# Scaling tokens by expert weights: one VectorE instruction per four tokens, named buffers, a fixed DMA order, and a first load split over two queues

## The chip, the cores and the metric

The kernel runs on one core of a Trainium2 chip. The metric is device time in microseconds (us) of one execution, as the median of several runs. The core's engines that matter here are VectorE (DVE in the profile), ScalarE (ACT) and SyncE (SP). ScalarE and SyncE also issue DMA transfers, each into a queue of its own; the transfers of both queues run on the core's 16 DMA engines.

## The reference, cut to what matters

```python
batch, seq, hidden, k = 16, 1024, 512, 2
# x: (16, 1024, 512) f32, expert_weights: (16, 1024, 2) f32; expert_indices is not used
x_expanded = x[:, :, np.newaxis, :].repeat(k, axis=2)
return (x_expanded * expert_weights[..., np.newaxis]).astype(np.float32)
```

There are 16,384 tokens of 512 numbers. Each token is written out twice, once times its first weight and once times its second. So 33.6 MB of x and 0.13 MB of weights are read, and 67.1 MB are written, with one multiplication for each number written.

## The kernel before, in words

**Tiling.** The 16,384 tokens are 128 per partition. They are taken in five groups of 24 tokens per partition and one of 8. Each group of 24 is cut into two tiles of 12 tokens, so there are eleven tiles, numbered 0 to 10 here: ten of 12 tokens per partition (3072 KB of x, 6144 KB of output) and a last one of 8 (2048 KB and 4096 KB). Inside a group a partition holds consecutive tokens, so that a tile's piece of x is 24,576 contiguous bytes per partition (16,384 in tile 10) and its output 49,152 (32,768 in tile 10).

**Buffers.** x has four buffers (`XB = 4`, line 31 and the pool in line 41), the output two (line 42). All weights lie in one tile, `w_tile`.

**Loads.** `load(i)` (lines 79 to 95) issues the load of tile i from ScalarE's queue. Tile 0 is cut into three pieces of four tokens (line 85), the others are one DMA each. After the first piece of tile 0 the weights of the first group are loaded (`first_weights`, line 56), and after its last piece all others (`other_weights`, lines 59 and 63). Lines 97 and 98 issue the loads of tiles 0 to 3 ahead. The load of tile i+4 stands in line 128, behind the work on tile i whose buffer it takes.

**Work.** For each token and each of its two weights there is one multiplication of 128x512 numbers by a scalar per partition: every third one goes to ScalarE (`nc.scalar.mul`, line 109), the other two to VectorE (`tensor_scalar`, line 115). That makes 85 on ScalarE and 171 on VectorE, 8 and 16 in a tile of 12 tokens.

**Stores.** When a tile is done, SyncE issues one store for it (line 124), eleven in all. An output buffer can be written again when the store before the last has landed.

**What sets the order.** The kernel is written with a layer that places each engine's instructions in an order of its own and adds the waits. Each engine and each queue then runs its instructions in that order: loads and ScalarE's multiplications share ScalarE's order, stores have SyncE's to themselves, and the order is not written by hand.

Of the kernel before, what the change touches and what calls it, by code (L numbers as in the profile page):

```python
# [1 line left out]

# [4 lines left out]


@with_exitstack
def kernel(  # L10
    ctx: ExitStack,
    tc: tile.TileContext,
    x: bass.AP,
    expert_indices: bass.AP,
    expert_weights: bass.AP,
    out: bass.AP,
):
    nc = tc.nc

    batch, seq, hidden = x.shape  # L20
    k = expert_weights.shape[-1]
    P = nc.NUM_PARTITIONS
    ntok = batch * seq
    assert ntok % P == 0
    A_TOTAL = ntok // P

    f32 = mybir.dt.float32
    row = k * hidden
    TX = 12
    TO = 12  # L30
    XB = 4

    groups = [[12, 12]] * 5 + [[8]]
    assert sum(sum(g) for g in groups) == A_TOTAL

    xf = x.rearrange("b s h -> (b s) h")
    of = out.rearrange("b s k h -> (b s) (k h)")
    wf = expert_weights.rearrange("b s k -> (b s) k")

    w_pool = ctx.enter_context(tc.tile_pool(name="w_pool", bufs=1))  # L40
    x_pool = ctx.enter_context(tc.tile_pool(name="x_pool", bufs=XB))
    o_pool = ctx.enter_context(tc.tile_pool(name="o_pool", bufs=2))

    w_tile = w_pool.tile([P, A_TOTAL * k], f32)

    def rows(of_all, done, T):
        return of_all[done * P : (done + T) * P, :].rearrange(
            "(p a) n -> p (a n)", a=T
        )

    T0 = sum(groups[0])
    G = len([g for g in groups[1:] if sum(g) == T0])
    head = (1 + G) * T0

    def first_weights():
        nc.scalar.dma_start(out=w_tile[:, : T0 * k], in_=rows(wf, 0, T0))  # L56

    def other_weights():
        nc.scalar.dma_start(  # L59
            out=w_tile[:, T0 * k : head * k].rearrange("p (g n) -> p g n", g=G),  # L60
            in_=wf[T0 * P : head * P, :].rearrange("(g p a) n -> p g (a n)", g=G, p=P),
        )
        nc.scalar.dma_start(  # L63
            out=w_tile[:, head * k :], in_=rows(wf, head, A_TOTAL - head)
        )

    tiles = []
    done = 0
    for group in groups:
        T = sum(group)  # L70
        a0 = 0
        for n in group:
            tiles.append((done, T, a0, n))
            a0 += n
        done += T

    loaded = []

    def load(i):
        if i >= len(tiles):  # L80
            return
        done, T, a0, n = tiles[i]
        x_tile = x_pool.tile([P, TX * hidden], f32)
        src = rows(xf, done, T)
        step = TX // 3 if i == 0 else n
        for at in range(0, n, step):
            nc.scalar.dma_start(  # L87
                out=x_tile[:, at * hidden : (at + step) * hidden],
                in_=src[:, (a0 + at) * hidden : (a0 + at + step) * hidden],
            )  # L90
            if i == 0 and at == 0:
                first_weights()
        if i == 0:
            other_weights()
        loaded.append(x_tile)

    for i in range(XB):
        load(i)
    for i, (done, T, a0, n) in enumerate(tiles):
        x_tile = loaded[i]  # L100
        outr = rows(of, done, T)
        for t in range(n):
            if t % TO == 0:
                o_tile = o_pool.tile([P, TO * row], f32)
            for kk in range(k):
                c = (done + a0 + t) * k + kk
                o = t % TO * row + kk * hidden
                if c % 3 == 2:
                    nc.scalar.mul(  # L109
                        out=o_tile[:, o : o + hidden],  # L110
                        in_=x_tile[:, t * hidden : (t + 1) * hidden],
                        mul=w_tile[:, c : c + 1],
                    )
                    continue
                nc.vector.tensor_scalar(  # L115
                    out=o_tile[:, o : o + hidden],
                    in0=x_tile[:, t * hidden : (t + 1) * hidden],
                    scalar1=w_tile[:, c : c + 1],
                    scalar2=None,
                    op0=mybir.AluOpType.mult,  # L120
                )
            if (t + 1) % TO == 0 or t + 1 == n:
                at = t // TO * TO
                nc.sync.dma_start(  # L124
                    out=outr[:, (a0 + at) * row : (a0 + t + 1) * row],
                    in_=o_tile[:, : (t + 1 - at) * row],
                )
        load(i + XB)

# [1 line left out]
_INS = ['x', 'expert_indices', 'expert_weights']  # L131
_OUTS = [((16, 1024, 2, 512), 'float32')]


# [23 lines left out]
```

## Time and profile before

| what | value |
|---|---|
| time, median of 3 runs | 240.93 us (240.92 to 242.47) |
| time of the profiled execution | 241.01 us |
| its span in the profile | 239.2 us (1.8 us lie around it) |
| VectorE busy | 68.8 us, 171 instructions |
| ScalarE busy | 54.7 us, 86 instructions (85 multiplications and a table load) |
| bytes moved by DMA | 100.82 MB, 421 GB/s over the span |
| loads of 3072 KB, issue to landing | 80.3 us (median of 9) |
| stores of 6144 KB, issue to landing | 31.4 us (median of 10) |

Times inside the profile are counted from the start of the span. The page gives busy times by engine, then the span in 40 slices with the mean busy share of the 16 DMA engines, then each DMA queue: q1 carries the stores that SyncE issues, q10 what ScalarE issues, and q14 is marked "instruction". A row of a group of instructions names its line, engine and operation, the shapes, the count, the busy time with the mean of one instruction in ns, and the idle time of that engine ahead of the instructions with what ended it. A row of the timeline has the start, how long the instructions from the first to the last took, the engine, the line and the count. "SPq" and "ACTq" are the queues' issuing instructions.

### The profile page before, as it was taken

What the parts mean: (1) busy time and instruction counts of PE and PEld (TensorE: products, weight loads), DVE (VectorE), ACT (ScalarE), POOL (GpSimd) and SP (SyncE); (2) the same over time, 40 slices, a digit from 0 to 9 for tenths busy, and PEclk for the clock granted to TensorE, in tenths of its full rate; (3) what the DMA queues carried; (4) which work ended last, traced back from release to release, by engine and by line L of the source; (5) the groups of instructions that cost most, each with busy time, mean ns of one, the idle gap of its engine ahead of it and who ended that gap; (6) DMA issues with size and microseconds to landing.
All of it is one profiled execution on the core that took longest, in us unless ns stands there. A gap on an engine that the chain in (4) does not pass through costs nothing.

```text
span 239.2 us, 378 instructions
## 1 busy us (share of the span) xinstructions
DVE 68.8 (29%) x171; ACT 54.7 (23%) x86; POOL 0.2 (0%) x4
## 2 busy tenths in 40 slices
DVE  0911900450082019004500820280055009107000
ACT  0911700430080016004300800260052008005000
POOL 0000000000000000000000000000000000000000
DMA  7999999999999989989999999999989998999994
GB/s 256 427 374 411 452 419 444 460 394 440 415 527 394 452 375 423 510 362 444 427 427 501 419 394 460 394 493 427 444 362 436 448 481 370 507 394 411 451 438 192
DMA packets 4275, 100.82 MB, mean 421 GB/s; under 512 B 1200, under 2 KB 1200, under 8 KB 1200
## 3 DMA queue, kind: packets, MB, share of 16 engines
q1 hardware_dynamic: 1584, 67.11, 64.8%
q10 hardware_dynamic: 2688, 33.69, 33.7%
q14 instruction: 3, 0.02, 0.0%
HBM read 33.69 MB, written 67.11 MB: 421 GB/s over the span
## 4 chain that ended last, share of the span: by engine, by line
DMA 56%; another core or an unknown queue 19%; DVE 15%; ACTq 1%; issue 0%; DVEq 0%; SPq 0%
DMA out_dram<-o_tile 39%; DMA x_tile<-in_x_dram 17%; DVE o_tile L115 15%; ACTq L87 1%; ACTq L63 0%; ACTq L59 0%; ACTq L56 0%; DVEq L115 0%; DVEq L153 0%; SPq L124 0%
## 5 line engine op out<-in xcount | busy, mean ns | idle before, releaser
L115 DVE TENSOR_SCALAR o_tile<-x_tile,w_tile 128x512 f32<-128x512 f32 x171 | 68.8, 482 | 152.7 <-DMA x_tile<-in_x_dram 146.8
L109 ACT ACTIVATE o_tile<-x_tile,w_tile 128x512 f32<-128x512 f32 x85 | 53.4, 708 | 159.5 <-DMA x_tile<-in_x_dram 159.5
L109 ACT ACT_TABLE_LOAD x1 | 1.3, 1283 | 6.0 <-DMA x_tile<-in_x_dram 6.0
L142 POOL MEMSET const-bfloat16-1.0<- 128x1 bf16 x1 | 0.1, 102 | 0.0
L142 POOL MEMSET const-uint8-127<- 128x1 uint8 x1 | 0.1, 101 | 0.0
L142 POOL MEMSET const-float32-0.0<- 128x1 f32 x1 | 0.1, 99 | 0.2 <-issue 0.2
L142 POOL MEMSET const-float32-1.0<- 128x1 f32 x1 | 0.1, 98 | 0.0
## 6 DMA issues: line engine op xcount, KB each, us to landing
out_dram<-o_tile SPq DMA_DIRECT2D x10, 6144.0 KB, 31.4
x_tile<-in_x_dram ACTq DMA_DIRECT2D x9, 3072.0 KB, 80.3
out_dram<-o_tile SPq DMA_DIRECT2D x1, 4096.0 KB, 16.7
x_tile<-in_x_dram ACTq DMA_DIRECT2D x3, 1024.0 KB, 6.6
x_tile<-in_x_dram ACTq DMA_DIRECT2D x1, 2048.0 KB, 78.0
w_tile<-in_expert_weights_dram ACTq DMA_DIRECT2D x1, 96.0 KB, 8.6
w_tile<-in_expert_weights_dram ACTq DMA_DIRECT2D x1, 24.0 KB, 4.7
w_tile<-in_expert_weights_dram ACTq DMA_DIRECT2D x1, 8.0 KB, 8.3
```

The lines of the kernel that those rows point to most:

```text
L87: nc.scalar.dma_start(out=x_tile[:, at * hidden : (at + step) * hidden], in_=src[:, (a0 + at) * hidden : (a0 + at + step) * hidden],)
L109: nc.scalar.mul(out=o_tile[:, o : o + hidden], in_=x_tile[:, t * hidden : (t + 1) * hidden], mul=w_tile[:, c : c + 1],)
L115: nc.vector.tensor_scalar(out=o_tile[:, o : o + hidden], in0=x_tile[:, t * hidden : (t + 1) * hidden], scalar1=w_tile[:, c : c + 1], scala ...
L142: nc = _bacc.Bacc("TRN2", target_bir_lowering=False, num_devices=1)
```

## The change

Four things are changed.

1. Tile 0 keeps its 24 single multiplications (`SINGLES = 1`). In tiles 1 to 10 nothing is multiplied on ScalarE, and VectorE works on four tokens at a time (`CH = 4`): one `tensor_tensor` takes 4 x 512 numbers of x, each read for both weights, and 8 weights, each read 512 times, and writes 4 x 2 x 512 = 4096 numbers per partition. There are three of these in a tile of 12 tokens and two in tile 10.
2. Every x buffer and every output buffer is a pool of its own, taken by tile number (`x_pools[i % XB]`, `o_pools[i % OB]`).
3. `tc.issue_after` keeps ScalarE's loads of x in the order of the program, each behind the one before it, and SyncE's stores likewise.
4. The first piece of tile 0 is two DMAs: partitions 0 to 63 from ScalarE's queue, 64 to 127 from SyncE's.

```diff
     TO = 12
     XB = 4
+    OB = 2
+    CH = 4
+    SINGLES = 1
...
-    x_pool = ctx.enter_context(tc.tile_pool(name="x_pool", bufs=XB))
-    o_pool = ctx.enter_context(tc.tile_pool(name="o_pool", bufs=2))
+    x_pools = [
+        ctx.enter_context(tc.tile_pool(name=f"x_pool{b}", bufs=1)) for b in range(XB)
+    ]
+    o_pools = [
+        ctx.enter_context(tc.tile_pool(name=f"o_pool{b}", bufs=1)) for b in range(OB)
+    ]
...
-            nc.scalar.dma_start(
-                out=x_tile[:, at * hidden : (at + step) * hidden],
-                in_=src[:, (a0 + at) * hidden : (a0 + at + step) * hidden],
-            )
+            dst = x_tile[:, at * hidden : (at + step) * hidden]
+            piece = src[:, (a0 + at) * hidden : (a0 + at + step) * hidden]
+            if i == 0 and at == 0:
+                H = P // 2
+                issued.append(nc.scalar.dma_start(out=dst[:H], in_=piece[:H]))
+                nc.sync.dma_start(out=dst[H:], in_=piece[H:])
+            else:
+                with tc.issue_after(issued[-1].ins):
+                    issued.append(nc.scalar.dma_start(out=dst, in_=piece))
...
-            for kk in range(k):
+            for kk in range(k if i < SINGLES else 0):
...
+            if i >= SINGLES and t % CH == 0:
+                c = (done + a0 + t) * k
+                o = t % TO * row
+                nc.vector.tensor_tensor(
+                    out=o_tile[:, o : o + CH * row].rearrange(
+                        "p (t k h) -> p t k h", t=CH, k=k
+                    ),
+                    in0=x_tile[:, t * hidden : (t + CH) * hidden]
+                    .rearrange("p (t h) -> p t h", t=CH)
+                    .unsqueeze(2)
+                    .to_broadcast([P, CH, k, hidden]),
+                    in1=w_tile[:, c : c + CH * k]
+                    .rearrange("p (t k) -> p t k", t=CH)
+                    .unsqueeze(3)
+                    .to_broadcast([P, CH, k, hidden]),
+                    op=mybir.AluOpType.mult,
+                )
...
-                nc.sync.dma_start(
-                    out=outr[:, (a0 + at) * row : (a0 + t + 1) * row],
-                    in_=o_tile[:, : (t + 1 - at) * row],
-                )
+                with tc.issue_after(stored.ins) if stored else ExitStack():
+                    stored = nc.sync.dma_start(
+                        out=outr[:, (a0 + at) * row : (a0 + t + 1) * row],
+                        in_=o_tile[:, : (t + 1 - at) * row],
+                    )
```

## The prediction

> **What bounds the kernel now.** I read the page's busy shares and slices first, then its DMA queues.
>
> ```profile
> span 239.2 us, 378 instructions
> DVE 68.8 (29%) x171; ACT 54.7 (23%) x86; POOL 0.2 (0%) x4
> ...
> DMA  7999999999999989989999999999989998999994
> ...
> q1 hardware_dynamic: 1584, 67.11, 64.8%
> q10 hardware_dynamic: 2688, 33.69, 33.7%
> q14 instruction: 3, 0.02, 0.0%
> HBM read 33.69 MB, written 67.11 MB: 421 GB/s over the span
> ...
> L115 DVE TENSOR_SCALAR o_tile<-x_tile,w_tile 128x512 f32<-128x512 f32 x171 | 68.8, 482 | 152.7 <-DMA x_tile<-in_x_dram 146.8
> L109 ACT ACTIVATE o_tile<-x_tile,w_tile 128x512 f32<-128x512 f32 x85 | 53.4, 708 | 159.5 <-DMA x_tile<-in_x_dram 159.5
> ```
>
> The two queues hold the 16 DMA engines for 64.8 + 33.7 = 98.5% of the span, 235.6 us. VectorE and ScalarE work for under a third of it and wait for loads. Then the table by stretches of the span (its last two columns are the DMA share and GB/s), to see where the other 1.5% lies:
>
> ```profile
> 0.00:1.00 1.00, 0.00 (x0) 0.00 (x0) 0.20 (x4) 1.00 0.00 0
> 1.00:2.00 1.00, 0.00 (x0) 0.00 (x0) 0.00 (x0) 1.00 0.56 98
> 2.00:3.00 1.00, 0.00 (x0) 0.00 (x0) 0.00 (x0) 1.00 0.70 229
> 3.00:5.00 2.00, 0.00 (x0) 0.00 (x0) 0.00 (x0) 1.00 0.99 396
> 5.00:65.00 60.00, 19.36 (x48) 16.42 (x25) 0.00 (x0) 1.00 1.02 429
> ...
> 185.00:217.00 32.00, 6.42 (x16) 5.01 (x8) 0.00 (x0) 1.00 1.02 439
> 217.00:236.00 19.00, 4.45 (x11) 3.17 (x5) 0.00 (x0) 1.00 0.99 426
> 236.00:237.00 1.00, 0.00 (x0) 0.00 (x0) 0.00 (x0) 1.00 0.08 33
> 237.00:239.20 2.20, 0.00 (x0) 0.00 (x0) 0.00 (x0) 1.00 0.00 0
> ```
>
> The engines are full from 3 to 236 us. What is not transfer lies at the two ends: 1.75 us until the first packet, about 0.6 us of slow start, and some 2 us behind the last packets. So the kernel is bound by its bytes, and an edit can gain only at the ends, or lose by letting the DMA engines run dry. The last view is the timeline (start, length, engine, line), for the instants at which work enters the queues late in the run:
>
> ```profile
> 197.80 6.42 DVE L115 TENSOR_SCALAR o_tile<-x_tile,w_tile 128x512 f32<-128x512 f32 x16 [15.33 <-DMA x_tile<-in_x_dram]
> 204.29 17.61 SPq L124 DMA_DIRECT2D out_dram<-o_tile  x2
> ...
> 217.06 4.45 DVE L115 TENSOR_SCALAR o_tile<-x_tile,w_tile 128x512 f32<-128x512 f32 x11 [12.84 <-DMA x_tile<-in_x_dram]
> ```
>
> Tile 9 is computed from 197.80 and stored at 204.29; tile 10 is there at 217.06 and stored at 221.57 (the second of the two stores). Tile 8's store, issued at 182.53, lands 29.54 us later at 212.07 in the chain of waits, so tile 9's store stands in the queue for some 8 us before it moves.
>
> **Four-token instructions: the count.** 155 of the 171 VectorE instructions and 77 of the 85 ScalarE ones go; 16 and 8 stay in tile 0. 9 x 3 + 2 = 29 instructions of 4096 results come. ScalarE falls to 8 x 0.708 + 1.3 = 7 us, and its loads no longer share its order with products of later tiles: the load of tile 4, issued at 23.20 behind such a product in the timeline, can go at about 13. That gains nothing, since tiles 0 to 3 (12.6 MB, 29 us at 429 GB/s) still fill the load queue.
>
> **Their price.** No row shows an instruction with two tensor operands. From below: VectorE's own row, 8 x 482 ns = 3.86 us for 4096 results. From above: ScalarE's row, 8 x 708 ns = 5.67 us, since a second operand may halve VectorE's rate but its fixed time is paid once instead of eight times. I take 4.4 us, nearer to VectorE's row, which is the same engine and the same number of results. A tile of 12 then takes 3 x 4.4 + 0.1 = 13.3 us instead of 6.42, tile 10 takes 8.9 instead of 4.45, and VectorE is busy 16 x 0.482 + 29 x 4.4 = 135 us, 57% of the span.
>
> **What hides it.** VectorE's work lies beside the transfers, so it costs nothing while a queue has packets. In the middle (tile 3's store goes out at 73.36 and lands at 105.13; tile 4's goes out at 95.50) each store is issued 9.6 us before the one ahead lands. A tile that takes 6.9 us longer leaves 2.7, less 1.06 from a store's issue to its first packet (13.03 to 14.09 in the packet records) and 0.45 from a last packet to the landing: about 1.2 us. If that runs out, three loads are queued and take the engines, the next tiles arrive earlier, and no transfer time is lost. Load i+4 waits for tile i's products and leaves 6.9 us later, 80 us before it lands: hidden as well. Late next is the output buffer: tile 5 starts at 110.72, and the buffer it needs is free at 105.13, so 5.6 us are left there.
>
> The cover is thin in one place, where the loads run out. Tile 8's store has its last byte at 212.07 - 0.45 = 211.6. Of tile 10's load (bytes from about 197.3 to 216.5, beside stores) a quarter, 0.53 MB, is then left; alone it takes 1.25 us, so the engines have work to 212.85. Tile 9's store is ready at 197.80 + 3C + 0.2 + 1.06 for an instruction of C us. With C = 4.4 that is 212.25: covered by 0.6 us. The limit is C = 4.6; at 5.67 it is ready at 216.05, and 3.2 us are lost. At 3.86 nothing is. For the last store, tile 10's x is then there by 213.3 and its products take 8.9: ready at 223.3, while tile 9's store moves until about 226.6 (the last store's 8 packets of 1.213 us on each engine end from 236.35 on). Cost taken: 0, bounds 0 and +3.2.
>
> [...]
>
> **Fewer instructions.** The page has three 8 KB packets of instruction loading on q14. The one at 222.0 us comes with a store packet of 2.17 us where the others take 1.82, and at the end 15 of the 16 engines finish between 236.35 and 237.15, one at 237.80. If fetches made that one late, removing over 200 of 378 instructions gives back 0 to 0.65 us. I take -0.35, one packet's delay.
>
> **Named buffers and fixed order.** The issues in the trace of before already follow the order of tiles, on both queues. Nothing moves; cost 0. If the order had to be bought by a wait, it would be on queues with 9.6 us (stores) and some 65 us (loads) in hand.
>
> **The split first piece.** One DMA more is issued, on SyncE, whose barrier ends at about 0.7 us like ScalarE's; issues take 0.33 to 0.59 us. Now the engines get their first packets from 1.75 to 2.23 us, in the order in which one issue (0.72 to 1.10) reaches them; two issues side by side could halve that spread, for -0.1 us on the mean and at most -0.48. From above: first packets take 0.47 to 1.19 us instead of 0.31, about +0.45 if each engine pays that twice. I take -0.1, because half the packets of each queue should go out in half the time. Queued behind on ScalarE are the weights and pieces 2 and 3, all with 31 us of cover. The load of tile 3, which went out at 5.66 behind the first piece's landing, and perhaps tile 2's, may now wait for the halves; tile 1 alone keeps the engines until 16 us. SyncE's first store is due at 13.03, long after.
>
> [...]
>
> **Sum**, against the profiled execution (241.01 = 239.2 + 1.8 around it; the median of the three is 240.93): 241.01 + 0 - 0.35 + 0 - 0.1 = 240.56, so 240.6 us.
>
> **Rivals.**
> 1. Bytes rule and the ends gain a little: 240.6. For it: DMA full from 3 to 236 us. Chance 0.55.
> 2. The edits at the ends do nothing: the late engine is late for another reason and the halves only interleave. 241.0. For it: the order was there already, and the first packets are slow whatever is queued. Chance 0.27.
> 3. Slower: VectorE's instruction takes over 4.6 us and the DMA engines run dry between the stores of tiles 8 and 9. At 5.67 us: 240.56 + 3.2 = 243.8. For it: no row shows the two-operand form. Against: VectorE's row would have to grow by a fifth, though fixed times are saved. Above 1% from about C = 5.5. Chance 0.14, of which 0.06 above 1%.
> 4. Faster by over 1%: the transfers themselves speed up with ScalarE silent. All at the best stretch's 439 GB/s would take 100.8 / 0.439 = 229.6 us instead of 236.05 - 1.75 = 234.3, so about 235.9. Against: the last stretch, with little compute, is at 426, and packets have one length (1.815 us for 48 KB). Chance 0.04.
>
> **How the numbers follow.** Within about 1% a measurement of this kernel cannot be told from no change (its three runs span 0.6%). Cases 1 and 2 and the small half of 3 lie within it: 0.55 + 0.27 + 0.08 = 0.90; slower 0.06, faster 0.04. The range goes from both ends gained in full, 241.01 - 0.65 - 0.48 = 239.9, to rival 3 at its bound, 243.8. The likeliest case's own range is 239.9 to 241.4.
>
> **What would show it.** Rows of the changed kernel: a two-operand VectorE group x29 at 3.9 to 4.6 us (above, rival 3); ScalarE's products x8; DMA slices full but for the two ends, queue shares near 235.6 us in sum, and no dip near 212 us; the q14 row with fewer than three packets; the first second of transfer no worse than 98 and 229 GB/s. A body rate off 429 GB/s, or an empty slice in the middle, would make the whole argument wrong.

## The result and the profile after

The changed kernel takes 242.01 us (median of 20 runs), the kernel before 241.0 us on the same chips: a ratio of 1.0037, 95% interval 1.0028 to 1.0046. The change costs 0.9 to 1.0 us. The prediction said 240.6, a small gain. The profiled execution took 242.07 us, with a span of 240.2, against 241.01 and 239.2.

Some executions of most kernels here, of both kernels of the change too, take 243 to 282 us, and in each of these that was profiled the DMA engines had fallen out of step (shown below); the ratios leave out what lies over 1.5% above the fastest of the same kernel, and e1, e3, e11 and e13, where all or nearly all executions were such, get none.

The page of the changed kernel, the lines that answer to those shown of before:

```profile
span 240.2 us, 157 instructions
DVE 133.1 (55%) x45; ACT 6.3 (3%) x9; POOL 0.2 (0%) x4
...
DMA  6999999999999999999999999999999999999996
...
q1 hardware_dynamic: 1664, 67.63, 65.4%
q10 hardware_dynamic: 2624, 33.16, 33.2%
HBM read 33.69 MB, written 67.11 MB: 420 GB/s over the span
...
L139 DVE TENSOR_TENSOR o_tile<-x_tile,w_tile 128x4096 f32<-128x4096 f32 x29 | 126.6, 4421 | 83.7 <-DMA x_tile<-in_x_dram 83.7
```

VectorE has nearly twice the work, 133.1 us, and still waits for loads. The new instruction takes 4.42 us. The queues hold the engines for 98.6% of a span that is 1 us longer: 236.8 us against 235.6 for the same bytes. So the engines were not idle more, they were slower. There is no q14 row any more.

Where they were slower shows in the table by stretches of the changed kernel (last column GB/s), with the same stretches as before:

```profile
1.00:2.00 1.00, 0.00 (x0) 0.00 (x0) 0.00 (x0) 1.00 0.00 0
2.00:3.00 1.00, 0.00 (x0) 0.00 (x0) 0.00 (x0) 1.00 0.92 221
3.00:5.00 2.00, 0.00 (x0) 0.00 (x0) 0.00 (x0) 1.00 1.04 250
5.00:65.00 60.00, 32.71 (x22) 6.29 (x9) 0.00 (x0) 1.00 1.02 423
...
217.00:236.00 19.00, 8.71 (x2) 0.00 (x0) 0.00 (x0) 1.00 1.01 436
236.00:237.00 1.00, 0.00 (x0) 0.00 (x0) 0.00 (x0) 1.00 1.14 492
```

At 3 to 5 us the engines are as busy as before (share 1.04), but move 250 GB/s instead of 396. Over the later stretches the rates come near those of before, and the end comes later: at 236 to 237 us, where the kernel before had 33 GB/s, there are still 492. Two stretches that isolate the place, first the kernel before, then the changed one:

```profile
3.00:8.00 5.00, 2.09 (x6) 1.97 (x3) 0.00 (x0) 1.00 1.00 410
14.00:20.00 6.00, 0.00 (x0) 0.00 (x0) 0.00 (x0) 1.00 1.05 373
```

```profile
3.00:8.00 5.00, 0.00 (x0) 0.00 (x0) 0.00 (x0) 1.00 1.02 223
14.00:20.00 6.00, 1.40 (x4) 1.50 (x3) 0.00 (x0) 1.00 1.12 483
```

The first 8 us are slow in the changed kernel, 14 to 20 us are slow in the kernel before. In the packet records, with each packet's bytes spread over its time, the change has moved 1.28 MB by 8 us and before 2.33: 1.05 MB less, 2.4 us at 433 GB/s. By 20 us the gap is 0.63 MB. About 1 us of the loss comes back there, because the kernel before has 29 load packets of 1.0 to 2.0 us instead of 0.91 just ahead of its first store packets, and the change has none there.

The slow packets are those of the split piece. In the changed kernel SyncE's 64 packets of 8 KB run from 2.04 to 4.91 us, ScalarE's 64 behind them from 3.91 to 7.22, though both were issued at 0.73; the later ones of each take 0.615 and 0.626 us in the median (0.31 is usual). So each half moves at half rate, and one after the other.

### The profile page after: what moved, and what is told of

Read it like the earlier page. It is cut to its first block, busy times and chain, and to the rows that moved or that the text cites. A ratio compares the mean times of both kernels' runs of the same rounds, so it can differ in the third digit from the quotient of the medians.

```text
span 240.2 us, 157 instructions
## 1 busy us (share of the span) xinstructions
DVE 133.1 (55%) x45; ACT 6.3 (3%) x9; POOL 0.2 (0%) x4
## 4 chain that ended last, share of the span: by engine, by line
DVE 45%; another core or an unknown queue 27%; DMA 19%; DVEq 2%; issue 0%
DVE o_tile L139 45%; DMA x_tile<-in_x_dram 19%; DVEq L185 2%; DVEq L139 0%
## 5 line engine op out<-in xcount | busy, mean ns | idle before, releaser
L139 DVE TENSOR_TENSOR o_tile<-x_tile,w_tile 128x4096 f32<-128x4096 f32 x29 | 126.6, 4421 | 83.7 <-DMA x_tile<-in_x_dram 83.7
L129 DVE TENSOR_SCALAR o_tile<-x_tile,w_tile 128x512 f32<-128x512 f32 x16 | 6.5, 482 | 8.9 <-DMA w_tile<-in_expert_weights_dram 8.6
L123 ACT ACTIVATE o_tile<-x_tile,w_tile 128x512 f32<-128x512 f32 x8 | 5.0, 708 | 0.0
```

Of the source, the lines that this page charges most:

```text
L123: nc.scalar.mul(out=o_tile[:, o : o + hidden], in_=x_tile[:, t * hidden : (t + 1) * hidden], mul=w_tile[:, c : c + 1],)
L129: nc.vector.tensor_scalar(out=o_tile[:, o : o + hidden], in0=x_tile[:, t * hidden : (t + 1) * hidden], scalar1=w_tile[:, c : c + 1], scala ...
L139: nc.vector.tensor_tensor(out=o_tile[:, o : o + CH * row].rearrange("p (t k h) -> p t k h", t=CH, k=k), in0=x_tile[:, t * hidden : (t + CH ...
```

## The experiments

Theory A: a load into 64 partitions that lie side by side moves at half rate (0.62 us a packet for 0.31), which costs the two halves 2.4 us, of which about 1 us comes back. Rival B: two queues that start together slow each other. Rival C: the four-token instructions cost the time. "Whole" below means that the first piece is again one DMA on ScalarE.

**e1: the change with a whole first piece.**

```diff
-                issued.append(nc.scalar.dma_start(out=dst[:H], in_=piece[:H]))
-                nc.sync.dma_start(out=dst[H:], in_=piece[H:])
+                issued.append(nc.scalar.dma_start(out=dst, in_=piece))
```

> The changed kernel with its first piece again one DMA of 128 partitions on ScalarE's queue; all else of the change stays. Theory A (a load into 64 adjacent partitions moves at half rate: its 8 KB packets took about 0.62 us instead of 0.31, which costs the two halves some 2.4 us, of which 1 us came back at 14 to 20 us): the stretch from 3 to 5 us is back near 396 GB/s, and the time is at or below the kernel before, 239.6 to 241.0. Rival B (two queues starting at once slow each other): the same, 239.6 to 241.0. Rival C (the four-token instructions cost the 0.9 us): 242.0, as the changed kernel.

Measured: 255.05 us, 250.35 to 259.16 in six runs. No theory had foreseen that. Its head is whole again (401 GB/s from 3 to 5 us), so A and B keep their first half; the loss comes later. Four stretches of e1, then the last two of them in the kernel before:

```profile
20.00:60.00 40.00, 26.19 (x6) 0.00 (x0) 0.00 (x0) 1.00 1.00 433
60.00:120.00 60.00, 35.20 (x9) 0.00 (x0) 0.00 (x0) 1.00 1.00 429
120.00:180.00 60.00, 30.32 (x8) 0.00 (x0) 0.00 (x0) 1.00 1.00 410
180.00:236.00 56.00, 34.91 (x8) 0.00 (x0) 0.00 (x0) 1.00 0.93 385
```

```profile
120.00:180.00 60.00, 16.80 (x42) 14.15 (x23) 0.00 (x0) 1.00 1.00 433
180.00:236.00 56.00, 13.34 (x34) 9.07 (x15) 0.00 (x0) 1.00 1.01 435
```

The rate falls step by step while the engines stay busy. In the packet records, store packets take up to 2.9 us instead of 1.82, and the 16 engines end one and the same store up to 11 us apart (tile 8's: 215.4 to 226.5), while the next step waits for the last. This is what "out of step" means here; it is taken up at e10.

**e2: the kernel before with the split alone.**

```diff
+                nc.scalar.dma_start(out=dst[:H], in_=piece[:H])
+                nc.sync.dma_start(out=dst[H:], in_=piece[H:])
```

> The kernel before with the split of the first piece (partitions 0 to 63 on ScalarE, 64 to 127 on SyncE) and nothing else of the change. Theory A and rival B: slower than before by 0.9 to 2.4 us, 242 to 243.4, with about 250 GB/s from 3 to 5 us. Rival C: 241.0, no change.

Measured: 242.52 us, ratio 1.0067 (1.0055 to 1.0079); 258 GB/s from 3 to 5 us:

```profile
3.00:5.00 2.00, 0.00 (x0) 0.00 (x0) 0.00 (x0) 1.00 1.03 258
```

The split alone costs 1.6 us, more than the whole change. Rival C falls: something else in the change gives about 0.5 us back.

**e3: the change with the first piece split by tokens, all 128 partitions in both halves.**

```diff
+                H = step * hidden // 2
+                issued.append(nc.scalar.dma_start(out=dst[:, :H], in_=piece[:, :H]))
+                nc.sync.dma_start(out=dst[:, H:], in_=piece[:, H:])
```

> The changed kernel with the first piece split by tokens in place of partitions: two of the four tokens on ScalarE's queue, two on SyncE's, each for all 128 partitions (4 KB packets). Theory A: the head is back near 390 GB/s from 3 to 5 us, time 239.6 to 241.0, as without a split. Rival B: still slow, 242. Rival C: 242.

Measured: 267.15 us, 257.96 to 276.97 in six runs: out of step, like e1. Its head still answers the question: 402 GB/s from 3 to 5 us, two queues at once.

```profile
3.00:5.00 2.00, 0.00 (x0) 0.00 (x0) 0.00 (x0) 1.00 1.02 402
```

Rival B falls; the time expected was missed.

**e4: the change with both partition halves on ScalarE's queue.**

```diff
+                issued.append(nc.scalar.dma_start(out=dst[:H], in_=piece[:H]))
+                nc.scalar.dma_start(out=dst[H:], in_=piece[H:])
```

> The changed kernel with both partition halves of the first piece on ScalarE's queue, one behind the other. Theory A: as slow as the change, 242, with 8 KB packets of about 0.6 us in the first 128. Rival B: back at 240 to 241. Rival C: 242.

Measured: six of twelve executions at 241.24 to 241.80 us, ratio 1.0023 (1.0012 to 1.0033), and six at 245.59 to 276.50. The profiled one, 241.44 us, has 258 GB/s from 3 to 5 us:

```profile
3.00:5.00 2.00, 0.00 (x0) 0.00 (x0) 0.00 (x0) 1.00 1.02 258
```

One queue, the same slow head: theory A, not B. It is some 0.5 us faster than the change and than expected; by 20 us it has moved 6.41 MB where the change has moved 6.28, about 0.3 us, and the rest is not explained. Why half of its executions are out of the range of the others was not tried.

**e5: the change with other halves, partitions 32 to 95 on SyncE and the outer quarters on ScalarE.**

```diff
+                Q = P // 4
+                nc.sync.dma_start(out=dst[Q : 3 * Q], in_=piece[Q : 3 * Q])
+                nc.scalar.dma_start(out=dst[:Q], in_=piece[:Q])
+                issued.append(nc.scalar.dma_start(out=dst[3 * Q :], in_=piece[3 * Q :]))
```

> The changed kernel with other halves: SyncE loads partitions 32 to 95 of the first piece, ScalarE 0 to 31 and then 96 to 127. [...] Theory A2 (any load of 64 partitions moves at half rate): all 128 packets near 0.6 us, time 242.

Measured: 240.86 us, with two of ten executions at 244.28 and 262.30; ratio 0.9978 (0.9948 to 1.0007), 1.2 us less than the change. The second 32 of SyncE's 64 packets take 0.313 us in the median, not 0.615. The stretches, to be held against the two pairs above:

```profile
3.00:8.00 5.00, 0.96 (x3) 0.89 (x1) 0.00 (x0) 1.00 1.01 318
14.00:20.00 6.00, 0.00 (x0) 0.00 (x0) 0.00 (x0) 1.00 1.07 459
```

So the 64 partitions in the middle come to the usual 0.31 us a packet, where the lower and the upper 64 took 0.62: theory A2 falls, and what decides is not the number of the partitions but which ones they are (theory A1). Of the 1.05 MB by which the change is behind at 8 us, e5 has made up 0.59, somewhat over half, and half of the piece's bytes go to the middle; by 20 us it is level with the kernel before (6.90 MB against 6.91). ScalarE's two quarters took 0.42 us a packet in the median, between the two.

**e6: the change with single multiplications in all tiles** (split, buffers and order stay).

```diff
-    SINGLES = 1
+    SINGLES = 11
```

> The changed kernel with single multiplications on VectorE and ScalarE in all tiles, as before: the split, the named buffers and the fixed order without the four-token instructions. If the four-token instructions bring the 0.7 us by which the change is faster than the split alone (fewer instructions to load, so that no engine ends late): as the split alone, 242.5, with three packets on q14 and its last landing 1.4 us behind the first engine's. If the order and the buffers bring it: 241.9.

Measured: 242.51 us, ratio 1.0061 (1.0045 to 1.0077), three packets on q14. That is the split alone (242.52): buffers and order bring nothing, the four-token instructions bring 0.5 us.

**e7: named buffers and fixed order alone.**

```diff
-    SINGLES = 1
+    SINGLES = 11
...
-                issued.append(nc.scalar.dma_start(out=dst[:H], in_=piece[:H]))
-                nc.sync.dma_start(out=dst[H:], in_=piece[H:])
+                issued.append(nc.scalar.dma_start(out=dst, in_=piece))
```

> The kernel before with named buffers and the fixed order alone. If they move nothing: 240.9, packets and stretches as before. If they are what spread the engines in the run with the whole first piece (255 us): 250 or more.

Measured: 240.95 us, ratio 0.9993 (0.9966 to 1.0019) and 397 GB/s from 3 to 5 us. The time does not move. With e6 this prices the split once more: 242.51 - 240.95 = 1.56 us.

**e8: whole first piece, one four-token instruction per tile, the rest single.**

```diff
-            for kk in range(k if i < SINGLES else 0):
+            for kk in range(k if i < SINGLES or t >= CH else 0):
...
-                if c % 3 == 2:
+                if c % 3 == 2 if i < SINGLES else c % 7 in (1, 3, 5):
...
-            if i >= SINGLES and t % CH == 0:
+            if i >= SINGLES and t == 0:
```

> Whole first piece, named buffers and fixed order, and in tiles 1 to 10 one four-token instruction for the first four tokens and single multiplications for the others, 9 or 10 on VectorE and 6 or 7 on ScalarE: some 9.1 us for a tile of 12 where the change takes 13.1 and the kernel before 6.4, and some 60 VectorE instructions fewer than before. If it is the length of a tile's products that lets the engines drift apart: no drift at 9.1 us, and 240.3 to 240.9 with fewer packets on q14. If it is the four-token instruction itself: 250 or more.

Measured: 240.22 us, with one of twelve executions at 278.56; ratio 0.9968 (0.9956 to 0.998): 0.7 us faster than the kernel before. The pages, e8 first and then e7:

```profile
span 238.4 us, 308 instructions
...
q14 instruction: 2, 0.02, 0.0%
```

```profile
span 239.3 us, 378 instructions
...
q14 instruction: 3, 0.02, 0.0%
```

In the packet records both have moved the same bytes at 8, 20 and 60 us (2.33 or 2.34, 6.95 and 24.29 MB), and 15 engines end their last store alike: 236.25 to 236.85 us in e7, 236.29 to 236.86 in e8. The sixteenth ends at 237.87 in e7, at 237.06 in e8. In e7, as in the kernel before, an instruction packet comes at 222.1 us with a store packet that is 0.35 us too long; e8 has none so late. The packet is not all of it in e7, where one engine is 1 us behind the others from tile 0's store on. The kernel before is clearer: tile 8's store ends on the 16 engines within 0.79 us (210.94 to 211.74), tile 9's, during which the packet at 222.0 comes, within 1.45 (226.66 to 228.11). The 0.66 us more is about the 0.31 of that packet and the 0.36 by which the store packet beside it is too long.

**e9: whole first piece, two four-token instructions per tile, ScalarE the last four tokens.**

```diff
-            for kk in range(k if i < SINGLES else 0):
+            for kk in range(k if i < SINGLES or t >= n - CH else 0):
...
-                if c % 3 == 2:
+                if c % 3 == 2 or i >= SINGLES:
...
-            if i >= SINGLES and t % CH == 0:
+            if i >= SINGLES and t % CH == 0 and t < n - CH:
```

> Whole first piece; in tiles 1 to 10 two four-token instructions on VectorE for the first eight tokens (one for the first four in tile 10) and single multiplications on ScalarE for the last four: 8.9 us for a tile of 12, with no single multiplication on VectorE. If the length of a tile's products makes the engines drift apart (255 us at 13.1 us, 240.2 at 9.1): no drift, 240.0 to 240.5. If it is the number of four-token instructions: 245 or more.

Measured: 240.37 us in the median of twelve executions, three of which took 249.76 to 278.43; ratio 0.9974 (0.9942 to 1.0006). The profiled one, 240.35 us, has one packet on q14 inside the run, and all 16 engines end between 236.23 and 236.77. Two four-token instructions a tile do no harm of the size of e1's.

**e10: e8 with the four-token instruction issued twice to the same place.**

```diff
-            if i >= SINGLES and t == 0:
+            for again in range(2 if i >= SINGLES and t == 0 else 0):
```

> The mixed kernel (one four-token instruction and 9 or 10 single multiplications on VectorE per tile) with the four-token instruction issued twice to the same place, so that a tile takes 13.5 us instead of 9.1 and no more of its results come from it. If the length makes the engines drift apart: 245 or more, with landings of one transfer spread over several us. If not: 240.2 to 240.5, as the mixed kernel.

Measured: 240.89 us, ratio 0.9996 (0.9961 to 1.003). A tile took 12.4 us, not 13.5. Six of ten executions took 240.01 to 240.90 us, four 243.60 to 263.14, so a tile of 12.4 us can keep the rate but does not always. The records of the profiled executions of e1 and e10 (240.88 us) part at one instant. Tile 1's store is issued at 36.23 us in e1 and at 35.51 in e10; tile 0's store ends on the engines from 38.5 to 39.0 in both. At 40.0 us all 16 engines are in a store packet in e10, but only 9 in e1: the others took another load packet. From there tile 2's load lands within 0.5 us on all engines in e10 (44.33 to 44.85) and spread over 2.4 us in e1 (42.45 to 44.84). That suggests theory D: a store that is issued too late misses its turn on some engines, and these run out of step with the rest. e10 is not wholly in step either: its tile 3's load lands over 1.8 us (64.82 to 66.58), and from tile 2's store on the last engine ends each store 1.2 us or more behind the first, the last store at 237.77 us, though no packet on q14 comes after 115.2.

**e11: e8 with one more small VectorE instruction per token.**

```diff
+    spare = w_pool.tile([P, 1], f32)
...
+            nc.vector.memset(spare, 0.0)
             if i >= SINGLES and t == 0:
```

> The mixed kernel with one more VectorE instruction per token, 128 in all, that clears one number per partition of a spare buffer: a tile takes about 1 us longer, and the number of instructions is again above that of before. If instruction loading delays the engine that ends last: more packets on q14 than the mixed kernel's two, and where two or more fall on one DMA engine its last packet ends 0.35 us later for each, 240.6 to 241.0. If not: 240.2.

Measured: 281.26 us, four runs from 245.25 to 282.36. The edit did not do what was meant: 34 of the added instructions run before tile 0's products, and tile 0's store is issued at 14.00 us instead of 12.99 (e8). In the profiled execution (282.36 us) the engines are out of step from that store on: at 18.5 us 7 of 16 are in a store packet where e8 has 16, and tile 1's load lands over 4.5 us (18.91 to 23.43). So it says nothing on instruction loading. That its first store comes too late, as theory D would have it, was not tried; it is left open.

**e12: e1 with tiles 0.9 us shorter** (the third instruction of a tile takes three tokens, ScalarE the last one).

```diff
-            for kk in range(k if i < SINGLES else 0):
+            for kk in range(k if i < SINGLES or t == n - 1 else 0):
...
-                if c % 3 == 2:
+                if c % 3 == 2 or i >= SINGLES:
...
+                m = min(CH, n - 1 - t)
```

> Whole first piece and the four-token instructions, 29 of them as in the run with the whole first piece (255 us), but the third of each tile takes three tokens and ScalarE multiplies the last one: 12.2 us for a tile of 12 instead of 13.1. Theory D (a store must be issued some 2.5 to 3 us before the one ahead ends, else some of the 16 engines miss their turn to start it, take a load in its place, and the engines fall out of step): tile 1's store is issued at 35.4 instead of 36.2, no engine misses its turn, tile 2's load lands on all 16 engines within 0.6 us instead of 2.4, and the time is 240.0 to 240.6. Rival (29 four-token instructions in a row as such, or the early load of tile 4, keep the engines out of step): 250 or more.

**e13: e9 made as long as e1.**

```diff
-            if i >= SINGLES and t % CH == 0 and t < n - CH:
+            for again in range(
+                (2 if t == 0 else 1) if i >= SINGLES and t % CH == 0 and t < n - CH else 0
+            ):
```

> The kernel with two four-token instructions and ScalarE's third (240.4 us at 8.9 us a tile), the first of them issued twice to the same place: 13.3 us a tile, and its time shows only what the length does. Theory D: tile 1's store is issued at 36.4, engines miss their turn, tile 2's load lands spread over 2 us or more, and later transfers are spread further: 245 or more, or at least 0.5 us above the shorter kernel. Rival: 240.4, landings within 0.6 us.

Measured: e12 240.7 us, ratio 0.9991 (0.9971 to 1.0011), the median slightly above what was expected, with one of ten executions at 252.46; e13 250.25, 260.79, 256.97 and 240.32 us. The timeline rows of tile 1's store, e12 and then e13:

```profile
35.24 0.34 SPq L155 DMA_DIRECT2D out_dram<-o_tile  x1
```

```profile
36.24 0.34 SPq L156 DMA_DIRECT2D out_dram<-o_tile  x1
```

One microsecond makes the difference here. In e12 all 16 engines are in a store packet at 40.0 us and tile 2's load lands from 44.26 to 44.87; in e13 12 are, and it lands from 42.47 to 44.80. e12 has as many two-operand instructions as e1, so their number is not the cause; e13 issues the load of tile 4 as late as e12 and the kernel before (23.1 us) and falls out of step all the same, so the early load is not either. What theory D said of these two kernels came out.

It is not the whole account. In the profiled executions of the changed kernel, e4 and e5, the same thing happens and heals: tile 2's load lands over 2.2 to 2.4 us (44.05 to 46.41 in the changed kernel), as in e1 and e13, but tile 3's within 1.0 us (65.85 to 66.84). In e1 and e13 it is 2.2 to 2.4 us again, and more later. And a few executions of the kernel before, whose tiles take 6.4 us, reach 250 us too. So in these profiles a late store makes engines miss their turn; why that grows in some kernels and heals in others, the runs do not show.

## Why the prediction was right and wrong

**The bound** was right. The transfers set the time in both kernels, with the engines held for 98.5% and 98.6% of the span; VectorE at 55% of the span still waits for loads (83.7 us). The price of the new instruction was right too (4.4 taken, 4.42 measured). The value from above, 5.67, allowed for a second operand that halves VectorE's rate; no run shows that: 4.42 us for 4096 results are 1.08 ns a result, the 482 ns of a single multiplication 0.94. A fixed time shows in e12, where 3072 results take 3.35 us and 4096 take 4.42: at that slope some 0.14 us do not grow with the length.

**"The split first piece" is the step that failed.** It was put at -0.1 us, between -0.48 and +0.45; it measured +1.56 (e6 against e7) and +1.6 (e2), so the time rose where a fall was forecast. The step assumed that half the packets go out in half the time, and took its upper end from the slow first packets. No row of before shows a load into half of the partitions, so the bound from 128-partition rows could not hold it: rate was the unknown, and all rows had the same. The runs show it: 215 to 252 GB/s in the changed kernel's packet records from 3.5 to 6 us, 258 GB/s from 3 to 5 us with both halves on one queue (e4), and 0.313 us for the later packets of the middle partitions (e5). Why the lower and the upper half move at half rate and the middle does not, no run shows. The prediction named the right rows to look at: the first microseconds of transfer, no worse than 98 and 229 GB/s, came out at 0 and 221, then 250 for 396.

**"Fewer instructions"** went the right way, and the records fit the reason given: without a late q14 packet, e8 and e9 have no late engine. The size was put at -0.35, with bounds 0 and -0.65; e8 measured -0.73 against e7. The step counted only the longer store packet (0.36 us), not the 0.31 us of the fetch itself. e10 shows that an engine can end late for another reason, and e12 that a late packet need not make one late: it has two (215.9 and 217.8), and its last store ends within 0.93 us. That two fetches land on the one engine that ends late is inferred from the lengths of its packets; e11, which was to double it, did not decide it. In the changed kernel only 0.5 us of it arrive (242.51 to 242.01). There, three load packets at 63.1 us take 1.41 to 1.52 us instead of 0.91, just where tile 1's store gives way to tile 2's, and from tile 2's store to the end three engines stay some 0.4 us behind the others (238.7 to 238.85 against 238.3 at the end). That the one causes the other fits these records but was not tried.

**"What hides it"** reached a cost of 0 with a wrong term: "1.06 from a store's issue to its first packet (13.03 to 14.09 in the packet records)". The records hold no store packet until 17.72 us: 4.7 us, in which all 16 engines are in load packets. So the 1.2 us said to be left in the middle did not exist; the changed kernel's tile 1 store, issued at 37.85, comes 2.1 to 2.7 us before tile 0's ends (39.95 to 40.55), and tile 2's load lands spread over 2.35 us. The step said that then "no transfer time is lost". In the changed kernel, 18 of 20 executions (241.59 to 242.21 us) bear that out. What the step left out is that 16 engines do not run dry at the same instant: they can fall out of step, and at 13.1 us a tile that cost 14 us in e1, at 12.2 us nothing in nine of ten executions of e12. That the changed kernel was spared is not explained, so here the cost of 0 was in part luck. The thin place between the stores of tiles 8 and 9, rival 3, did not open: the slices stay full.

**"Named buffers and fixed order"** at 0 was right (e7: -0.06 us against before, within its interval).

**The sum** as measured: +1.56 for the split, 0 for buffers and order, -0.5 for the four-token instructions, together +1.06; the kernels differ by 1.01. (e6 stands in the first and the last of these differences, so this is no check of its own; e2, with +1.6 for the split alone, is one.) None of the four rivals was this case.

## What to carry to other kernels

The DMA engines were held for 98.6% of the changed kernel's span, and the split's price of 1.6 us lay in a rate, not in idle time: where they are as full, check for every new or reshaped transfer that some row shows its shape, above all the partitions that it spans, and count it at half rate if it spans only the lower or the upper half (0.62 us for an 8 KB packet here, not 0.31). Read the time from a store's issue to its first packet from the packet records, not from the issue. Watch how long before the end of the store ahead each store is issued: with a whole first piece, 3.2 us or more kept the engines in step in e12's profile, 2.2 to 2.8 us did not in e1's and e13's. Try to save instructions without making a tile late: e8, with 308 for 378, took 240.22 us, and no fetch came late on the engine that ended last.

## What the runs showed of the hardware that was not expected

- Loads into partitions 0 to 63 or 64 to 127 moved 8 KB packets in 0.62 us (the changed kernel, the later ones of each half), into 32 to 95 in 0.31 (e5, the second 32 packets), into all in 0.31 (the kernel before).
- Two halves issued in the same instant from two queues went one behind the other: SyncE's first packet at 2.04 us, ScalarE's at 3.91. Two halves by tokens (e3) landed side by side, at 4.83 to 5.45 and 5.01 to 5.64.
- The first store packet came 4.7 us after its issue when loads were queued (13.03 to 17.72).
- Around one 8 KB packet of instruction loading at 222.0 us, the spread of the engines' ends grew by 0.66 us: 0.31 is its own time, 0.36 the store packet beside it.
- 16 DMA engines that fell out of step drifted further apart: in e1 tile 2's load lands over 2.4 us, tile 6's over 7.9, and tile 8's store ends on the engines 11 us apart, with packets of up to 2.9 us for 1.82; e1 took 250 us and more. In the changed kernel the spread of tile 2's load was gone with tile 3's. Why it heals there, why e11 starts it with its first store, and why a first piece split by partitions removes the slow packets at 14 to 17 us, is open.
